# An encoder step in float32: right sides of three norms built between the sums of the next pair, a phase's first factors applied at the end of its first unit

## The chip, the cores and the metric

One core of a Trainium2 chip runs the whole program. The metric is the device time of one execution in microseconds, the median over several. Lower is better. The engines are TensorE (PE), VectorE (DVE), ScalarE (ACT), GpSimd (POOL), and SyncE (SP), whose queue issues all transfers between DRAM and the on-chip memory, in order.

## The reference

One inference step of a four-layer trunk for 1024 prompt tokens and 8 × 16 sample tokens, 1152 columns together, D = 1024 rows, all in float32. After the attention layer (its output projection is `w_ao`) the same residual `x` goes through a feed-forward layer, a gated short convolution and another feed-forward layer:

```python
def swiglu(h, wg, wu, wd):
    return (jax.nn.silu(h @ wg) * (h @ wu)) @ wd

def conv_mixer(h, w_in, conv_w, w_out, conv_state):
    gate_b, gate_c, u = jnp.split(h @ w_in, 3, axis=-1)
    xin = gate_c * u
    ...
    y = (gate_b * conv) @ w_out

xp = xp + mp                                          # attention or conv
xp = xp + swiglu(rms_norm(xp, norm_ffn[i]), w_ffn_gate[i], w_ffn_up[i], w_ffn_down[i])
```

`rms_norm` multiplies each column by the root of its mean square's inverse, and each row by a gain.

## The kernel before

**Products.** Every float32 factor is split into a high and a low half (`part`, `halve`: ScalarE casts the high half, VectorE subtracts it to get the low one), and a product is three matmuls: high by high, high by low, low by high. `x` lies as eight tiles of 128 x 1152 (rows by columns), `x[0]` to `x[7]`. A matmul has 384 columns (a third of a tile) or 288 (a quarter).

**Phases.** After attention come, in this order: the last chunk of the output projection (`pairs` with `w_aol`, two of the heads), `gates` of layer 0 (22 units), `down` of layer 0, `conv` (12 units), `w_cout` (`down` again), `gates` of layer 1, `down_last`. `gates` and `conv` write their results `y` to DRAM (`yd`), and the `down` phases load them back in chunks: DOWN = (2, 8, 8, 4) and COUT = (2, 2, 4) blocks of 128 rows of `y` per chunk. In a chunk `pairs` goes through four pairs of `x` tiles, (0, 4), (1, 5), (2, 6), (3, 7); for each of six groups (two tiles, three thirds) TensorE sums nk products, three matmuls each, and VectorE adds the group to `x` (L1130).

**Units.** A unit (`unit`) is a 2 x 2 block product done with seven products instead of eight. Each has a left side from the weights (`a11`, `s1` to `s4` and so on) and a right side from `x` (`t1` to `t4`, `b11`, `b21`, `b22`; a trace calls them tt1, tb11 and so on with h or l for the half), in the order t2, t1, b11, b21, t3, t4, b22. Each is 24 matmuls of 288 columns, 12 for each half `s`, 168 in a unit. Right sides are built once per phase, and all units use them. There are 28 slots for halves (NT = 20 of their own and NY = 8 shared with `y`).

**A norm.** In the last chunk before `gates` or `conv`, `sides(st, x, j)` is called after each pair: it builds that pair's share of the right sides from `x` (ScalarE `v`, VectorE L899 and L869), and squares both tiles in halves of 576 columns (ScalarE L932), which GpSimd adds to `ssq` (L933). Sides without a free slot go to `late` and are built in `end_sides`. The norm's factor is not in the right sides; it is a row `rb`, multiplied into the products (`first`, `second` and `end` in the callback `sink`). `rb` comes from `sums` (18 small matmuls over `ssq`), `rstd` (a chain of some 15 short VectorE instructions) and `spread`: high diagonals from ScalarE (L276), low ones from GpSimd (L278), 18 matmuls of 384 columns, three copies.

**What sets the order.** The program is recorded through a scheduling layer, which may exchange neighbours on an engine; then each engine runs its own list in order. `tick` is called after each half of a product and runs what `late` holds when its count of ticks is over: `sums` two ticks into the first unit, `spread` three later, so ahead of the unit's first use of `rb`:

```python
        self.late.append([2, sums])
        ...
            self.late.append([3, lambda: spread(r)])
```

**The names around it.** `g` and `u` of a unit come from rings of three buffers (`wide`, ZBUFS = 3). `row` gives full-width rows from a ring of three. `xd` is `x` in DRAM: `x` is spilled there before `conv`, since `conv` uses the `x` buffers for `xi`, and loaded back for `w_cout` (L1206). A `conv` unit's channel ends with three taps and `cv` times `rb` (L1094, GpSimd, 128 x 1152).

## Time and profile before

| what | value |
|---|---|
| time, median of 3 runs | 2751.44 us (2749.30 to 2755.26) |
| profiled execution, its own time | 2751.61 us |
| its span | 2749.5 us |
| TensorE busy | 2623.1 us, 95% |
| VectorE busy | 1736.9 us, 63% |
| ScalarE busy | 929.4 us, 34% |
| GpSimd busy | 660.4 us, 24% |
| mean granted TensorE clock | 0.975 |
| DMA | 276.28 MB, mean 100 GB/s |

The profiled execution's time is 2.1 us more than the span from its first to its last instruction. Busy shares are means over phases of different kinds; the granted clock is a share of the full 2.4 GHz, so 0.5 is the lower level of 1.2 GHz. Matmuls overlap in the records, so a pace is read from start to start or from counts in a stretch.

### The profile page before, as it was taken

The page shows a single profiled execution, that of the slowest core. Times are in us where ns is not written, and L with a number is a line of the kernel's source. Part 1 is how long each engine was busy: PE and PEld are TensorE (multiplying, and loading weights), DVE is VectorE, ACT ScalarE, POOL GpSimd, SP SyncE. Part 2 cuts the span into 40 slices and gives each one's busy share as a digit, 9 for nine tenths or more (in the row PEclk, how much of TensorE's full clock was granted, in tenths as well). Part 3 has the DMA queues.
Part 4 walks back from the last instruction along what each step waited for, and adds up shares of the span by engine and source line. Part 5 has one row for each costly group of instructions (what it writes and reads, how often), then busy time and mean ns, then how long its engine had stood idle before and what let it go on. Part 6 is the DMA issues. An engine that isn't in the chain of part 4 may idle for free. (4 is left out here: it accounts for less than half of the span.)

```text
span 2749.5 us, 45135 instructions
## 1 busy us (share of the span) xinstructions
PE 2623.1 (95%) x17440; PEld 2575.7 (94%) x17440; DVE 1736.9 (63%) x3535; ACT 929.4 (34%) x1765; POOL 660.4 (24%) x699
## 2 busy tenths in 40 slices
PE   7999999999599999999999799989899999999998
PEld 6899999989599999999999799989799999999997
DVE  7667766687866666665327776677766666673325
ACT  5555444453422222232104321223422222241114
POOL 6334233320322222220002333321322222220002
PEclk9999999999799999999999899999899999999999
DMA  6655555561022222244212122261122222253211
GB/s 195 181 170 167 165 179 172 162 215 42 20 93 73 76 73 79 76 134 138 72 39 90 37 78 61 65 186 30 41 88 75 74 73 73 76 174 95 72 39 69
DMA packets 176952, 276.28 MB, mean 100 GB/s; under 512 B 38241, under 2 KB 107745, under 8 KB 176737
## 3 DMA queue, kind: packets, MB, share of 16 engines
q1 hardware_dynamic: 176736, 273.40, 32.0%
q8 instruction: 137, 2.24, 0.3%
q14 instruction: 79, 0.64, 0.1%
HBM read 201.95 MB, written 71.38 MB: 99 GB/s over the span
## 5 line engine op out<-in xcount | busy, mean ns | idle before, releaser
L868 ACT CAST h<-r 128x512 fp32r<-128x512 f32 x492 | 302.9, 617 | 999.8 <-PE ps_g L996 457.3
L869 DVE TENSOR_TENSOR l<-r,h 128x512 fp32r<-128x512 f32 x492 | 348.5, 709 | 119.5 <-ACT h L868 104.6
L163 PE MATMUL ps_g<-yh,h 128*128 128x384 f32 x1152 | 387.2, 336 | 3.8 <-DVE g L1015 3.8
L164 PE MATMUL ps_g<-yl,h 128*128 128x384 f32 x1152 | 387.9, 337 | 0.0
L165 PE MATMUL ps_g<-yh,l 128*128 128x384 f32 x1152 | 386.0, 335 | 0.0
L1041 POOL TENSOR_TENSOR u<-u,rb 128x576 f32<-128x576 f32 x88 | 146.9, 1670 | 665.7 <-DVE u L999 658.4
L1130 DVE TENSOR_TENSOR x<-ps_g,x 128x384 f32<-128x384 f32 x264 | 141.6, 553 | 237.0 <-PE ps_g L165 236.8
L163 PEld LDWEIGHTS ps_g<-yh,h 128*128 128x128 f32 x1152 | 216.7, 188 | 5.0 <-DVE g L1015 4.7
L165 PEld LDWEIGHTS ps_g<-yh,l 128*128 128x128 f32 x1152 | 216.6, 188 | 0.0
L164 PEld LDWEIGHTS ps_g<-yl,h 128*128 128x128 f32 x1152 | 216.4, 188 | 0.0
L163 PE MATMUL ps_g<-hh,wh 128*128 128x384 f32 x544 | 193.8, 357 | 10.1 <-ACT hh L197 6.7
L967 DVE TENSOR_TENSOR r<-r,r 128x512 f32<-128x512 f32 x224 | 174.8, 780 | 40.6 <-DMA r<-in_w_gu 19.2
L164 PE MATMUL ps_g<-hl,wh 128*128 128x384 f32 x544 | 185.7, 341 | 1.5 <-DVE hl L198 1.4
L165 PE MATMUL ps_g<-hh,wl 128*128 128x384 f32 x544 | 185.1, 340 | 0.8 <-DVE wl L155 0.8
L933 POOL TENSOR_TENSOR ssq<-ssq,sq 128x576 f32<-128x576 f32 x42 | 75.6, 1821 | 409.4 <-ACT sq L932 409.3
L1045 DVE TENSOR_TENSOR g<-g,u 128x576 f32<-128x576 f32 x88 | 67.1, 762 | 143.1 <-ACT g L1044 143.0
L995 PE MATMUL ps_g<-tb21h,h 128*128 128x288 f32 x448 | 137.0, 306 | 18.7 <-ACT u L1002 18.7
L995 PE MATMUL ps_g<-tt2h,h 128*128 128x288 f32 x448 | 133.1, 298 | 9.9 <-ACT tt2h L868 9.9
L997 PE MATMUL ps_g<-tb21h,l 128*128 128x288 f32 x448 | 137.1, 306 | 0.0
L996 PE MATMUL ps_g<-tb21l,h 128*128 128x288 f32 x448 | 136.6, 305 | 0.0
L995 PE MATMUL ps_g<-tt3h,h 128*128 128x288 f32 x448 | 135.2, 302 | 1.2 <-DVE g L1003 1.2
L995 PE MATMUL ps_g<-tt1h,h 128*128 128x288 f32 x448 | 133.6, 298 | 1.5 <-ACT tt1h L868 1.5
(277 smaller groups left out, 7555.7 us busy)
## 6 DMA issues: line engine op xcount, KB each, us to landing
r<-in_w_gu SPq DMA_DIRECT2D x176, 256.0 KB, 2.7
y<-yd SPq DMA_DIRECT2D x52, 576.0 KB, 4.6
yd<-g SPq DMA_DIRECT2D x96, 288.0 KB, 2.6
r<-in_w_down SPq DMA_DIRECT2D x88, 256.0 KB, 2.6
wr<-in_w_in SPq DMA_DIRECT2D x24, 512.0 KB, 4.2
r<-in_w_cin SPq DMA_DIRECT2D x48, 256.0 KB, 2.7
kc<-in_ck SPq DMA_DIRECT2D x16, 512.0 KB, 4.3
vc<-in_cv SPq DMA_DIRECT2D x16, 512.0 KB, 4.0
```

Source lines behind the costliest of these rows:

```text
L163: nc.tensor.matmul(ps, wh, xh, start=(j == 0), stop=False)
L164: nc.tensor.matmul(ps, wh, xl, start=False, stop=False)
L165: nc.tensor.matmul(ps, wl, xh, start=False, stop=(j == n - 1))
L868: self.nc.scalar.copy(hi, raw)
L869: self.nc.vector.tensor_tensor(lo, raw, hi.bitcast(F32), ALU.subtract)
L933: nc.gpsimd.tensor_tensor(st["ssq"][:, cs], st["ssq"][:, cs], sq, ALU.add)
L967: nc.vector.tensor_tensor(t, x_, y, ALU.add)
L995: nc.tensor.matmul(ps, w[0][:, k, :], hi, start=(new and k == 0), stop=False, skip_group_check=True)
L996: nc.tensor.matmul(ps, w[0][:, k, :], lo, start=False, stop=False, skip_group_check=True)
L997: nc.tensor.matmul(ps, w[1][:, k, :], hi, start=False, stop=(k == 3), skip_group_check=True)
L1041: nc.gpsimd.tensor_tensor(u, u, self.cols(rb, s), ALU.mult)
L1130: nc.vector.tensor_tensor(x[m][:, c], ps, x[m][:, c], ALU.add)
```

## The change

Six edits; names and lines are those of the changed kernel where it is spoken of alone.

1. `sides` builds nothing at once. It returns three lists: `now` (sides that have slots), `then` (sides without) and squares. `pairs` runs `now`, and the squares of the pair before, in portions after each of the next pair's six adds. What is left is run after the last pair, sides first, squares last.
2. `square` squares a whole tile (128 x 1152) on ScalarE, and VectorE adds it to `ssq`; GpSimd's 14 half adds of each norm are gone.
3. `sums` comes six ticks into the phase; then 18 diagonals are made in one go into two rows, and `spread` comes at tick 15, which is in the second unit. The first unit (`first`) therefore doesn't use `rb`: ScalarE copies its product instead, and `rest` multiplies `g` (VectorE) and `u` (GpSimd) by `rb` after the spread and then runs the unit's `end`.
4. The first unit begins with those products that don't need the last pair's sides (three of four k blocks of t2 and t1, two of four of b11: 48 matmuls). Its left sides are built before the last pair's right sides. The first pair of a norm's chunk runs all its `y` but the last first, for its six groups.
5. The chunks: `w_ao[0]` (heads 0 and 1 of the second map) is no longer a separate accumulation but part of `w_aol`, which now has four blocks; layer 0's `down` has (2, 6, 8, 6), layer 1's stays; `w_cout` has (2, 6). NY is 11 and NT 17, the same 28 slots.
6. `x` is spilled to `xd` in the chunk before `gates` of layer 1, too. Where `x` is spilled, its tiles 0, 4, 1 and 5 become slots for right sides as soon as their own sides are built; `fetch_x` loads `x` back before `w_cout` and before `down_last`, in the order 0, 4, 1, 5, 2, 6, 3, 7.

The conv unit's and the gate's callbacks (`sink`) become functions `end` that run after both halves are multiplied; both of the gate's writes to `yd` now stand there. In the diff a line that is only "..." marks what is left out.

```diff
-NY = 8
+NY = 11
-DOWN = (2, 8, 8, 4)
-COUT = (2, 2, 4)
+DOWN = ((2, 6, 8, 6), (2, 8, 8, 4))
+COUT = (2, 6)
-NT = 20
+NT = 17
-SUMS = 5
+SUMS = 6
+SPREAD = 15
...
-        y0 = heads(self.od[0], (0, 1))
+        y = heads(self.od[0], (0, 1))
         self.accumulate(pp, x, y1, i["w_ao"][3], step=loom.step)
         loom.drain()
-        y1 = heads(self.od[0], (2, 3))
-        self.accumulate(pp, x, y0, i["w_ao"][0], banks="gs")
+        y += heads(self.od[0], (2, 3))
...
+        now = [lambda: vee("v"), one, two, lambda: halve("t2", "r2"), lambda: halve("t1", "r1"), four, lambda: halve("t4", "r4")]
...
             if self.side(st, p, z) is not None:
-                do()
+                now.append(do)
             else:
-                st["late"].append(do)
...
-                    sq = flat("zu", "sq")
-                    nc.scalar.activation(sq, xm[:, cs], AF.Square)
-                    nc.gpsimd.tensor_tensor(st["ssq"][:, cs], st["ssq"][:, cs], sq, ALU.add)
...
+            sq = self.row("sq")
+            nc.scalar.activation(sq, xm, AF.Square)
+            nc.vector.tensor_tensor(st["ssq"], st["ssq"], sq, ALU.add)
+
+    def roots(self, st):
...
+            dg = [self.row("diag", F32R) for _ in range(2)]
+            for j in range(9):
+                c = slice(j * P, (j + 1) * P)
+                nc.scalar.activation(dg[0][:, c], self.ident, AF.Copy, scale=parts[:, 0, j:j + 1].bitcast(F32))
+                nc.gpsimd.tensor_scalar(dg[1][:, c], self.ident, parts[:, 1, j:j + 1].bitcast(F32), 1.0, ALU.mult, ALU.mult)
+            self.late.append([SPREAD - SUMS, lambda: spread(dg)])
...
+            for do in st["rest"]:
+                do(rb)
+        self.late.append([SUMS, sums])
...
+        if first:
+            for n in range(3):
+                for s in range(2):
+                    products(n, s, range(2 if n == 2 else 3))
...
+                    if first:
+                        nc.scalar.copy(zg[s][:, 0], ps)
+                    else:
+                        vt.tensor_tensor(zg[s][:, 0], ps, by()[0][:, self.head(s)], ALU.mult)
...
+        if first:
+            def rest(s, rb):
+                nc.vector.tensor_tensor(zg[s], zg[s], self.cols(rb, s), ALU.mult)
+                nc.gpsimd.tensor_tensor(zu[s], zu[s], self.cols(rb, s), ALU.mult)
+                end(s, zg[s], zu[s])
...
+            early = nk - 1 if st is not None and j == 0 else 0
+            if early:
+                for g in groups:
+                    products(*g, range(early))
+            for n, (z, b, ps) in enumerate(groups):
+                products(z, b, ps, range(early, nk))
+                self.tick()
+                c = slice(b * BLK, (b + 1) * BLK)
+                xm = x[j + 4 * z][:, c]
+                nc.vector.tensor_tensor(xm, ps, xm, ALU.add)
+                for _ in range(-(-len(todo) // (6 - n))):
+                    todo.pop(0)()
             if st is not None:
-                self.sides(st, x, j)
+                if j == KT // 2 - 1:
+                    st["split"] = self.left_sides(*st["first"])
+                now, late, square = self.sides(st, x, j)
+                if st["spill"] and j < 2:
+                    self.free += ["x", "x"]
+                squares.append(square)
+                todo = now + (squares.pop(0) if j or st["spill"] else [])
+                then.append(late)
...
+    def fetch_x(self):
+        self.free = [t for t in self.free if t != "x"]
+        x = [self.xtile("x") for m in range(KT)]
+        for j in range(KT // 2):
+            for m in (j, j + 4):
+                self.nc.sync.dma_start(x[m], self.xd[m])
+        return x
...
-            st = self.begin_sides(3, pp, False)
+            st = self.begin_sides(3, pp, gu(1)(0), True)
             self.down(pp, x, i["w_cout"], COUT, st)
-            self.gates(pp, 1, st)
-            self.down_last(pp, x, i["w_down"][1], DOWN)
+            self.gates(pp, gu(1), st)
+            x = self.fetch_x()
+            self.down_last(pp, x, i["w_down"][1], DOWN[1])
```

What the scheduling layer makes of it is seen in the lists of the engines. First VectorE, norm 1, at the last pair of the last chunk, before the change (`x_1701` and `x_1705` are the tiles 3 and 7, `ps_g` a group's sum, `r` an intermediate, `tt` and `tb` right sides):

```order
L1130 TENSOR_TENSOR x_1701_7325<-ps_g_9028,x_1701_7325 128x384
L869 TENSOR_TENSOR tt1l_8985<-r_2081_8990,tt1h_8984 128x576
L1130 TENSOR_TENSOR x_1701_7325<-ps_g_9036,x_1701_7325 128x384
L869 TENSOR_TENSOR tt4l_8987<-r_2083_8994,tt4h_8986 128x576
L1130 TENSOR_TENSOR x_1701_7325<-ps_g_9044,x_1701_7325 128x384
L1130 TENSOR_TENSOR x_1705_7329<-ps_g_9052,x_1705_7329 128x384
L1130 TENSOR_TENSOR x_1705_7329<-ps_g_9060,x_1705_7329 128x384
L1130 TENSOR_TENSOR x_1705_7329<-ps_g_9068,x_1705_7329 128x384
L899 SCALAR_TENSOR_TENSOR r_2102_9078<-x_1701_7325,gains,v_9076 128x576
L899 SCALAR_TENSOR_TENSOR tb11l_9003<-x_1701_7325,gains,tb11h_9002 128x576
L899 SCALAR_TENSOR_TENSOR r_2103_9080<-x_1705_7329,gainsn,r_2102_9078 128x576
```

The same place after the change (`r_9020` and the like are left sides of the first unit, `l_9025` a low half of one):

```order
L1183 TENSOR_TENSOR x_1701_7325<-ps_g_8912,x_1701_7325 128x384
L869 TENSOR_TENSOR tt1l_8895<-r_2073_8931,tt1h_8894 128x576
L990 TENSOR_TENSOR r_9020<-r_9016,r_9018 128x512
L1183 TENSOR_TENSOR x_1705_7329<-ps_g_8913,x_1705_7329 128x384
L869 TENSOR_TENSOR tt4l_8897<-r_2075_8965,tt4h_8896 128x576
L990 TENSOR_TENSOR r_9022<-r_9014,r_9016 128x512
L1183 TENSOR_TENSOR x_1705_7329<-ps_g_8914,x_1705_7329 128x384
L869 TENSOR_TENSOR l_9025<-r_9020,h_9024 128x512
L990 TENSOR_TENSOR r_9028<-r_9022,r_9018 128x512
L898 SCALAR_TENSOR_TENSOR r_2097_9052<-x_1701_7325,gains,v_9050 128x576
L1183 TENSOR_TENSOR x_1705_7329<-ps_g_8915,x_1705_7329 128x384
```

Right sides of the pair before and left sides of the unit now stand between the adds of the last pair.

GpSimd from the last `ssq` adds of norm 1 to the second half of the first unit, before:

```order
L933 TENSOR_TENSOR ssq_8829<-ssq_8829,sq_9100 128x576
L933 TENSOR_TENSOR ssq_8829<-ssq_8829,sq_9103 128x576
L278 TENSOR_SCALAR diag_9264<-ident,rp_9257 128x128 x3
L278 TENSOR_SCALAR diag_9279<-ident,rp_9272 128x128 x3
L278 TENSOR_SCALAR diag_9294<-ident,rp_9287 128x128 x3
L1041 TENSOR_TENSOR u_9303<-u_9303,rb_9122 128x576
L1041 TENSOR_TENSOR u_9320<-u_9320,rb_9122 128x576
```

And after the change, in the first and second unit (`u_9189`, `u_9247` are the first unit's, `u_9489` the second's):

```order
L967 TENSOR_SCALAR diag_9227<-ident,rp_2132_9223 128x128 x9
L1078 TENSOR_TENSOR u_9189<-u_9189,rb_9405 128x576
L1078 TENSOR_TENSOR u_9247<-u_9247,rb_9405 128x576
L1062 TENSOR_TENSOR u_9489<-u_9489,rb_9405 128x576
L1062 TENSOR_TENSOR u_9506<-u_9506,rb_9405 128x576
```

The adds are gone, the nine low diagonals stand together, and the first unit's products follow them instead of standing in its middle.

SP's queue where `conv` ends and `w_cout` begins, before (`y` loads from `yd`, `x` from `xd`):

```order
L1206 DMA x_20069<-xd 128x1152
L1206 DMA x_20070<-xd 128x1152
L858 DMA r_20255<-in_w_cout 128x512
L1114 DMA y_20311<-yd 128x1152
L1114 DMA y_20317<-yd 128x1152
L858 DMA r_20321<-in_w_cout 128x512
L1103 DMA yd<-u_19931 256x1x288
L858 DMA r_20375<-in_w_cout 128x512
L1103 DMA yd<-u_19948 256x1x288
L1206 DMA x_20071<-xd 128x1152
L1106 DMA yd<-g_19930 256x1x288
```

And after the change:

```order
L1217 DMA x_19982<-xd 128x1152
L1217 DMA x_19986<-xd 128x1152
L858 DMA r_20171<-in_w_cout 128x512
L1153 DMA y_20239<-yd 128x1152
L1153 DMA y_20245<-yd 128x1152
L858 DMA r_20261<-in_w_cout 128x512
L858 DMA r_20267<-in_w_cout 128x512
L858 DMA r_20273<-in_w_cout 128x512
L1217 DMA x_19983<-xd 128x1152
L1145 DMA yd<-u_19847 256x1x288
L1145 DMA yd<-u_19864 256x1x288
```

Four `x` loads instead of six stand ahead of the first two `y`, and the last `y` writes stand together.

## Rows read from the trace of the kernel before

**Rows 1.** The page: busy time, share of the span and instructions by engine.

```profile
PE 2623.1 (95%) x17440; PEld 2575.7 (94%) x17440; DVE 1736.9 (63%) x3535; ACT 929.4 (34%) x1765; POOL 660.4 (24%) x699
```

**Rows 2.** Stretches: length, busy time of each engine (instructions), TensorE clock, DMA share, GB/s.

```profile
645.30:669.30 24.00, 24.00 (x141) 24.00 (x140) 15.67 (x29) 2.53 (x4) 0.00 (x0) 1.00 0.23 77
669.30:727.00 57.70, 31.81 (x163) 30.36 (x161) 56.67 (x74) 33.59 (x53) 24.76 (x14) 0.76 0.03 10
...
761.00:783.20 22.20, 22.20 (x170) 22.20 (x169) 14.31 (x25) 6.30 (x11) 4.82 (x5) 1.00 0.32 101
1507.60:1556.60 49.00, 35.32 (x193) 33.11 (x192) 34.57 (x62) 20.91 (x40) 17.14 (x17) 0.76 0.14 50
...
1936.70:1984.60 47.90, 34.78 (x195) 32.29 (x194) 35.37 (x63) 20.02 (x39) 17.87 (x18) 0.79 0.11 33
```

**Rows 3.** Timeline, TensorE, norm 1: start, length, instruction, idle before and releaser.

```profile
699.02 0.66 PE L163 MATMUL ps_g<-oh,h 128*128 128x384 f32 x1 [9.39 <-DVE x L1130]
...
723.15 1.01 PE L948 MATMUL ps_n<-ones,ssq 128*128 128x1 f32 x4 [15.66 <-POOL ssq L933]
```

**Rows 4.** Timeline, TensorE, norm 2 (the first three) and norm 3.

```profile
1518.20 0.85 PE L995 MATMUL ps_g<-tt2h,h 128*128 128x288 f32 x2 [4.95 <-ACT tt2h L868]
...
1524.67 0.49 PE L948 MATMUL ps_n<-ones,ssq 128*128 128x1 f32 x3 [1.54 <-POOL ssq L933]
...
1537.60 0.69 PE L286 MATMUL ps_n<-diag,onesr 128*128 128x384 f32 x1 [4.37 <-ACT diag L276]
...
1966.57 0.69 PE L286 MATMUL ps_n<-diag,onesr 128*128 128x384 f32 x1 [4.27 <-ACT diag L276]
```

**Rows 5.** Timeline, GpSimd, the last sums of squares of norm 1.

```profile
717.40 7.51 POOL L933 TENSOR_TENSOR ssq<-ssq,sq 128x576 f32<-128x576 f32 x4 [3.44 <-ACT sq L932]
```

**Rows 6.** Groups of VectorE by shape: count, busy us, mean ns, idle before.

```profile
L869 DVE TENSOR_TENSOR l<-r,h 128x512 fp32r<-128x512 f32 x492 | 348.5, 709 | 119.5 <-ACT h L868 104.6
...
L1130 DVE TENSOR_TENSOR x<-ps_g,x 128x384 f32<-128x384 f32 x264 | 141.6, 553 | 237.0 <-PE ps_g L165 236.8
...
L869 DVE TENSOR_TENSOR yl<-y,yh 128x1152 fp32r<-128x1152 f32 x52 | 72.7, 1403 | 27.4 <-ACT yh L868 27.4
...
L899 DVE SCALAR_TENSOR_TENSOR r<-x,gainsn,r 128x576 f32<-128x576 f32 x24 | 19.4, 809 | 0.0
...
L869 DVE TENSOR_TENSOR tt2l<-r,tt2h 128x576 fp32r<-128x576 f32 x12 | 9.0, 749 | 0.0
```

**Rows 7.** Timeline, VectorE, sides of norm 1.

```profile
694.58 1.95 DVE L899 SCALAR_TENSOR_TENSOR r<-x,gains,v 128x576 f32<-128x576 f32 x1
...
728.12 1.53 DVE L899 SCALAR_TENSOR_TENSOR tb22l<-x,gains,tb22h 128x576 fp32r<-128x576 f32 x2
```

**Rows 8.** Timeline, GpSimd, low diagonals of norm 1.

```profile
739.82 2.99 POOL L278 TENSOR_SCALAR diag<-ident,rp 128x128 fp32r<-128x128 f32 x6 [14.91 <-DVE rp L269]
744.17 1.06 POOL L278 TENSOR_SCALAR diag<-ident,rp 128x128 fp32r<-128x128 f32 x3 [1.35 <-PE ps_n L286]
```

**Rows 9.** Timeline, VectorE, GpSimd and TensorE, the second chain of conv.

```profile
1592.29 3.03 DVE L967 TENSOR_TENSOR r<-r,r 128x512 f32<-128x512 f32 x1
...
1591.73 3.04 POOL L1094 TENSOR_TENSOR cv<-cv,rb 128x1152 f32<-128x1152 f32 x1 [2.84 <-DVE cv L1093]
...
1596.38 0.40 PE L995 MATMUL ps_g<-tb21h,h 128*128 128x288 f32 x1 [2.15 <-ACT u L1002]
...
1598.05 0.44 PE L996 MATMUL ps_g<-tb21l,h 128*128 128x288 f32 x1
1598.29 0.44 PE L997 MATMUL ps_g<-tb21h,l 128*128 128x288 f32 x1
```

**Rows 10.** Waits of TensorE, 1580 to 1870 us: in total, times, longest us.

```profile
PE ps_g L995 <- ACT u L1002: 12.8, 6, 2.2
```

**Rows 11.** Timeline, TensorE, beginning of `w_cout`.

```profile
1837.47 0.44 PE L163 MATMUL ps_g<-yh,h 128*128 128x384 f32 x1 [2.22 <-DVE g L1015]
```

**Rows 12.** DMA issues, 1810 to 1840 us: count, KB each, median us to landing.

```profile
x<-xd SPq DMA_DIRECT2D x7, 576.0 KB, 12.7
```

More of the change, by code (lines that the diff above doesn't have):

```diff
@@ L218, in norm_sum @@
                 self.norm_end(st, b)()
-            elif st["new"] is not None:
-                self.late.append([SUMS, lambda: self.late.append([1, self.norm_end(st, b)])])
             elif b < NB - 1:
@@ L869, in halve, with begin_sides @@
         self.nc.vector.tensor_tensor(lo, raw, hi.bitcast(F32), ALU.subtract)
-    def begin_sides(self, gi, pp, spill):
-        return {"gi": gi, "pp": pp, "t": {}, "late": [], "ssq": None, "spill": spill, "v": {}}
+    def begin_sides(self, gi, pp, first, spill=False):
+        return {"gi": gi, "pp": pp, "t": {}, "ssq": None, "first": first, "spill": spill, "split": None, "rest": None}
     def side(self, st, p, z, need=False):
@@ L981, in unit, with products @@
         for n in range(PARTS):
-            if order[n][0] in raws:
-                split[order[n][0]] = self.part(raws[order[n][0]])
-        zone = {}
-        zg, zu = [None, None], [None, None]
+            wn = self.ORDER[n][0]
+            if wn in raws:
+                split[wn] = self.part(raws[wn])
+        return split, raws
+    def unit(self, pp, st, weights, by, end, last=False):
+        nc = self.nc
+        first = "rb" not in st
+        if st["split"] is not None:
+            split, raws = st["split"]
+            st["split"] = None
+        else:
+            split, raws = self.left_sides(*weights)
+        order = self.ORDER
+        zone, zg, zu = {}, [None, None], [None, None]
+        tail = lambda s: slice(HALF + s * SUB, HALF + (s + 1) * SUB)
+        vt = nc.vector
+        neg = lambda t, z: vt.scalar_tensor_tensor(t, z, -1.0, t, ALU.mult, ALU.subtract)
+        def products(n, s, ks):
+            wn, p, zn = order[n]
+            w = split[wn]
+            new = (zn, s) not in zone
+            if new:
+                zone[zn, s] = self.psum(pp, "g", (P, 512))[:, :SUB]
+            ps = zone[zn, s]
+            for k in ks:
+                hi, lo = (t[:, k % 2, s * SUB:(s + 1) * SUB] for t in self.side(st, p, k // 2))
+                nc.tensor.matmul(ps, w[0][:, k, :], hi, start=(new and k == 0), stop=False, skip_group_check=True)
+                nc.tensor.matmul(ps, w[0][:, k, :], lo, start=False, stop=False, skip_group_check=True)
+                nc.tensor.matmul(ps, w[1][:, k, :], hi, start=False, stop=(k == 3), skip_group_check=True)
+        if first:
+            for n in range(3):
+                for s in range(2):
+                    products(n, s, range(2 if n == 2 else 3))
@@ L986, in unit @@
         for n, (wn, p, zn) in enumerate(order):
-            w = split[wn]
             for s in range(2):
-                new = (zn, s) not in zone
-                if new:
-                    zone[zn, s] = self.psum(pp, "g", (P, 512))[:, :SUB]
+                products(n, s, range(4) if not first or n > 2 else range(2 if n == 2 else 3, 4))
                 ps = zone[zn, s]
-                for k in range(4):
-                    hi, lo = (t[:, k % 2, s * SUB:(s + 1) * SUB] for t in self.side(st, p, k // 2))
-                    nc.tensor.matmul(ps, w[0][:, k, :], hi, start=(new and k == 0), stop=False, skip_group_check=True)
-                    nc.tensor.matmul(ps, w[0][:, k, :], lo, start=False, stop=False, skip_group_check=True)
-                    nc.tensor.matmul(ps, w[1][:, k, :], hi, start=False, stop=(k == 3), skip_group_check=True)
@@ L1022, in unit @@
                 split[ahead] = self.part(raws[ahead])
+        if first:
[3 more added lines that the diff above has]
+                end(s, zg[s], zu[s])
+            st["rest"] = [lambda rb, s=s: rest(s, rb) for s in range(2)]
+            st["rb"] = None
     def cols(self, t, s):
@@ L1135, in pairs @@
         if st is not None:
-            self.end_sides(st)
+            names = [p for p, _ in then[-1]]
+            for p in names:
+                for late in then:
+                    for q, do in late:
+                        if q == p:
+                            do()
+            for square in squares:
+                for do in square:
+                    do()
+            self.roots(st)
+    def fetch_x(self):
[5 more added lines that the diff above has]
+        return x
     def down(self, pp, x, wsrc, chunks, st):
@@ L1317 @@
         o[name] = nc.dram_tensor(f"out_{name}", shape, F32, kind="ExternalOutput").ap()
-    i["w_down"] = [[i[f"w_down{l}{n}"] for n in range(len(DOWN))] for l in range(2)]
+    i["w_down"] = [[i[f"w_down{l}{n}"] for n in range(len(DOWN[l]))] for l in range(2)]
     i["w_cout"] = [i[f"w_cout{n}"] for n in range(len(COUT))]
```

222 lines of the change are left out of this document (106 added, 116 removed).

## The prediction

> **What bounds the kernel now.** I read the page's busy times first: TensorE is busy 95% of the span [rows 1], so time can only be won where it stands or runs at half clock. The table of stretches shows where [rows 2]. The stretch from 645.3 is a steady one: 139 matmuls of 384 columns (two of the 141 counted began earlier) in 24.0 us, 0.174 us each; a whole unit of gates (168 matmuls of 288 columns) takes the 22.2 us from 761.0, 0.132 us each, both at clock 1.00. At this pace a phase's first unit needs 22.2 us, 3.1 us for the 18 matmuls of `spread` and about 2 us for the sums, 27.3 in all. The three changes of phase need far more:
> - Norm 1 (the chunk `w_aol` from 669.3 to the end of the first unit at 761.0): 91.7 us for 144 × 0.174 + 27.3 = 52.4, an excess of 39.3.
> - Norm 2 (1507.6 to 1556.6): 49.0 for 27.3, excess 21.7.
> - Norm 3 (1936.7 to 1984.6): 47.9 for 27.3, excess 20.6.
>
> Together 81.6 us; half clock (0.76 to 0.79 mean in these rows) is part of it. The waits say what is late. In norm 1 TensorE stands 9.39 us for the add of `x`, which VectorE has queued behind right sides, and 15.66 us for the last GpSimd add of `ssq` [rows 3]. In norm 2 it stands 4.95 us for `tt2h` of the last pair and 4.37 for the diagonals, in norm 3 4.27 for the diagonals [rows 4]. GpSimd's adds follow one another, four in 7.51 us [rows 5], and beside them a VectorE side takes 1.95 us [rows 7] where its group's mean is 0.81 [rows 6].
>
> **The change, part by part.** The profiled run took 2751.61 us, 2.1 above its span and 0.2 above the median of 2751.44, so the sum is made from 2751.6.
>
> *Norm 1.* The two heads of `w_ao[0]` join the last chunk: 144 matmuls move from ahead of it into it, so it begins at 645.3 and has 288 matmuls, 50.1 us. Three of four heads run first for pair 0, so the first `x` add comes after 57 matmuls, at 655.2; from then on VectorE is the one to count. Between its first add and the last `ssq` add the new order has 24 adds of 0.553 us, 28 sides of 0.809, 16 halves of 0.749, 8 of 0.709, 4 left-side adds near 0.709 and 7 `ssq` adds of 128x1152, for which I take the 1.403 of the equally wide `yl` [rows 6]: 13.3 + 22.7 + 12.0 + 5.7 + 2.8 + 9.8 = 66.3 us. These are durations of single instructions; back to back they start closer (two sides in 1.53 us [rows 7]), which makes it about 60. So `ssq` is done at 715 to 721. TensorE could be there at 645.3 + 50.1 + 96 × 0.132 = 708.1. It will stand 7 to 13 us before or at the sums, and behind them in its order stands the rest of the unit. I take 8, near the lower end: the means of [rows 6] hold cases that a GpSimd add slowed, and no such add is left. The diagonals come next: from the sums VectorE's root chain, with what is interleaved, is some 10 us by the same prices, then nine high diagonals on ScalarE and, beside them and longer, nine low ones on GpSimd (six in 2.99 us [rows 8]): 4.5 us more. Their `spread` now stands 85 matmuls (11.2 us) later, against the 11.9 us that sums to spread took in norm 2 [rows 4]. So about 2.5 us of wait is left, and I add 2.5 us of half clock for both (1.5 follow a wait of 2.15 us in the conv phase, below). Excess 13 instead of 39.3: a gain of 26.3. Bounds: excess 6 (all at the lower prices, no half clock) to 25.
>
> *Norms 2 and 3.* The last chunk has six `y` (before: four), 108 matmuls or 18.8 us per pair. VectorE's same 66 us now lie beside 75 us of pairs and the 12.7 us up to the sums, no longer behind them. Of the last pair only `tt2`, `tt1` and `b11` are on the path: from its last add some six instructions, 5.3 us, against 48 matmuls of cover (6.3 us). If that cover is gone, each us late is a us lost. Left are about 2.5 us at the spread and 1.5 of half clock, excess 4 each (1 to 12): gains 17.7 and 16.6.
>
> *First unit's factors at its end.* `g` times `rb` (two of 576 on VectorE), `u` times `rb` (two on GpSimd): they stand beside second-unit work on engines that are idle a third of a unit (VectorE 14.3 busy of 22.2 us [rows 2]). They cost nothing unless the three buffers of `g` and `u` run out: the fourth is wanted after six groups of the second unit, and the first is freed earlier by two or three us, by my count. Cost 0, bound 3 us a phase.
>
> *Conv.* The chains `cv` times `rb` stay on GpSimd: 3.04 us there, 3.03 for the left-side add on VectorE beside it, ScalarE's `u` stands behind that add's half, and TensorE waits 2.15 us and then runs at half clock for some 3 us (0.24 us from start to start in place of 0.13) [rows 9], about 1.5 us lost; 12.8 us of wait in six such places [rows 10]. A seventh, the first, lies at 1566. The diff leaves the order of the six; the first chain now follows the second unit's spread and may lie elsewhere: gain 0 to 3.7, I take 2.
>
> *x through DRAM.* Eight loads before `w_cout` as before, now four of them behind the first `y` pair; so the 2.22 us that TensorE stands there [rows 11] stay, within ±6; price 0. For `w_down` 1 eight more loads and for norm 3 eight writes: four loads stand early in the gates, four among the `y` loads at the end. In a crowd a load lands after 12.7 us [rows 12], and what is behind it in SP's queue is late by its start; I take 2 us of loss (0 to 6).
>
> *One fewer chunk in `w_cout`, 24 fewer adds in each of two places*: VectorE work beside a busy TensorE; nothing.
>
> Sum: −26.3 − 17.7 − 16.6 − 2 + 0 + 2 = −60.6, so 2751.6 − 60.6 = **2691 us**. Norm 1's 8 us is the softest term.
>
> **A rule weighed.** The rows: six low diagonals on GpSimd took 2.99 us beside VectorE's adds, 0.50 us each; three in 1.06 us are 0.35 each [rows 8]; and a two-input add beside a GpSimd product took 3.03 [rows 9]. The Trainium skill (SBUF — State Buffer, "Who interferes with whom") says that a VectorE instruction with two SBUF inputs and a GpSimd instruction that reads SBUF exclude each other for the whole instruction. The product's row agrees; the diagonals' row does not show a whole wait for each. By that row the sum stays 2691; whole waits are the second rival.
>
> **Rivals.**
> - *VectorE becomes the bound inside the pairs.* Sides now stand between the adds that free TensorE's banks; before, such a queue cost 9.39 us once [rows 3]. For it: in norm 1 60 to 66 us of VectorE work meet 53 us of TensorE. Against: norms 2 and 3 have 88 us. If every pair is late, excesses of 25, 12 and 12: gain 14.3 + 9.7 + 8.6 = 32.6, about 2719.
> - *Low diagonals late.* If each of the nine waits for one VectorE instruction of 0.749 [rows 6], they take 9 × (0.35 + 0.75) = 9.9 instead of 4.5 us: 5.4 us more at each spread, 16 in all, 2707. For it rows 9, against it rows 8. This is what the rule named above would do.
> - *More is won.* Excesses of 6, 1, 1 and the first conv chain gone: gain 33.3 + 20.7 + 19.6 + 3.7 − 2 = 75, 2676.
> - *Slower.* A load of `x` waits in SP's queue until a side slot is free, and weights and `y` stand behind it in order. Side slots in `x` buffers come free only in a phase's last unit. If the queue stands so before `w_cout` and `w_down`, TensorE waits for `y`. The price is up to a unit (22.2 us) for each of the two; to outweigh 60 us of gain it must be three units or more. Against it: the loads that stand early need other buffers.
>
> **How the numbers follow.** Forecast 0.60, VectorE the bound 0.19, low diagonals 0.09, more won 0.06, slower 0.04, a gain lost to several of these so that it lies within 0.2% (5.5 us, about what a measurement of this kernel can tell) 0.02. The likeliest, with norm 1 between its bounds and the others in the middle, lies between 2684 and 2703; the range of 2668 to 2720 takes in the first three rivals, and below them the 6 us of `w_cout`. Faster 0.94, same 0.02, slower 0.04.
>
> **What would show it.** Right: no GpSimd add of `ssq`, sides at 0.7 to 0.8 us throughout, one wait of 7 to 13 us near the sums of norm 1, in norms 2 and 3 no wait for `tt2h` and a few us at the diagonals, six conv waits of 2 us left. Wrong: waits for `x` adds inside the pairs, for `u` or `g` buffers in second units, or for `y` behind `x` loads.

## The result

The changed kernel takes 2702.37 us, the kernel before 2751.96 us beside it; 49.6 us less by the medians; the ratio, taken over all runs, is 0.9815 with a 95% interval of 0.9802 to 0.9828. The forecast was 2691. A second timing of the same kernel on another chip (the run "again" below) gave 0.9785 (0.9764 to 0.9805), so a kernel's ratio is known to about 0.3% only, and small edits are read from stretches of the profile rather than from the total.

The page's busy line of the changed kernel:

```profile
PE 2609.2 (97%) x17440; PEld 2568.3 (95%) x17440; DVE 1715.0 (64%) x3498; ACT 935.1 (35%) x1761; POOL 581.2 (22%) x651
```

TensorE is busy for 14 us less than in [rows 1] in a span that is 50.3 us shorter. The stretches that answer to [rows 2]: from attention's last matmul to the third unit of norm 1, the first two units of norm 2, the other nine of `conv` up to the last, the last `conv` unit with `w_cout`, and the first three units of norm 3:

```profile
645.00:761.70 116.70, 102.55 (x651) 100.83 (x650) 92.92 (x156) 58.30 (x94) 11.77 (x14) 0.94 0.20 63
1486.30:1540.30 54.00, 49.96 (x361) 49.16 (x360) 46.03 (x84) 21.01 (x43) 16.99 (x18) 0.97 0.18 52
1540.30:1766.20 225.90, 211.38 (x1515) 209.75 (x1514) 164.16 (x263) 47.48 (x83) 70.42 (x60) 0.95 0.24 69
1766.20:1897.70 131.50, 125.80 (x747) 125.05 (x746) 92.97 (x141) 46.60 (x66) 15.16 (x9) 0.97 0.42 135
1897.70:1978.00 80.30, 74.59 (x530) 73.93 (x530) 55.73 (x103) 30.84 (x58) 16.36 (x18) 0.94 0.33 108
```

The same stretches of the kernel before took 139.1, 75.3, 223.9, 129.9 and 92.4 us. So norm 1 gave 22.4 us, norm 2 21.3 and norm 3 12.1; `conv` and `w_cout` took 2.0 and 1.6 back, the end 0.8, and the parts ahead of norm 1 and between norms 1 and 2 together 1.1. In norms 2 and 3 the first units alone take 24.3 us each, where [rows 2] has 49.0 and 47.9; the units behind them take 3.5 us (norm 2) and 11.4 us (norm 3) longer than before, of which 1.1 each is the `spread` that moved there. The waits of TensorE in the span (in total, times, longest us) show what is left:

```profile
PE ps_g L1033 <- ACT u L1048: 22.2, 12, 2.2
PE ps_g L1170 <- ACT h L868: 9.3, 1, 9.3
PE ps_g L1033 <- DVE u L1057: 7.6, 4, 3.9
...
PE ps_g L1033 <- DVE u L1022: 4.5, 1, 4.5
...
PE ps_g L1034 <- DVE tb11l L898: 1.8, 1, 1.8
```

No wait for `ssq`, for a diagonal of these norms or for `tt2h` is left; those for 9.39 and 15.66 us of [rows 3] and for 4.95, 4.37 and 4.27 of [rows 4] are gone. In their place stand 9.3 us at the beginning of norm 1, 3.9 and 2.9 us in second units, and 4.5 us at the end of `conv`.

**The new wait of norm 1.** SP's queue in the timeline, then TensorE's first matmul of the merged chunk:

```profile
646.64 0.45 SPq L570 DMA_DIRECT2D o<-olo  x1
648.91 0.80 SPq L790 DMA_DIRECT2D o<-o  x2
649.82 7.13 SPq L858 DMA_DIRECT2D r<-in_w_aol  x8
```

```profile
654.60 0.69 PE L1170 MATMUL ps_g<-oh,h 128*128 128x384 f32 x1 [9.32 <-ACT h L868]
```

The chunk's weights (`in_w_aol`) are issued behind the transfers of the last heads, which wait for attention's end. Before, 24 us of matmuls of `w_ao[0]` stood between; now nothing does, and TensorE waits for the high halves of the weights.

**VectorE in norm 1.** Its first add and its last `ssq` add:

```profile
666.61 3.16 DVE L1183 TENSOR_TENSOR x<-ps_g,x 128x384 f32<-128x384 f32 x6 [8.70 <-PE ps_g L1172]
...
724.89 1.34 DVE L949 TENSOR_TENSOR ssq<-ssq,sq 128x1152 f32<-128x1152 f32 x1
```

From 666.6 to 726.2 are 59.6 us, where the prediction had 60 to 66. No side is slowed beside them now: two take 1.53 us throughout.

**The new wait of norm 3.** ScalarE, then VectorE, then TensorE in the second unit of layer 1's gates (its third begins at 1952.1):

```profile
1940.26 1.15 ACT L868 CAST yh<-y 128x1152 fp32r<-128x1152 f32 x1 [6.45 <-DMA y<-yd]
```

```profile
1941.44 1.36 DVE L869 TENSOR_TENSOR yl<-y,yh 128x1152 fp32r<-128x1152 f32 x1 [4.83 <-ACT yh L868]
1942.72 0.45 DVE L1057 TENSOR_TENSOR u<-ps_g,u 128x288 f32<-128x288 f32 x1
```

```profile
1943.22 0.61 PE L1033 MATMUL ps_g<-tt4h,h 128*128 128x288 f32 x1 [3.92 <-DVE u L1057]
```

ScalarE stands 6.45 us at the cast of a `y` that is still on its way from DRAM, VectorE behind it at that cast's low half, and the `u` that frees TensorE's bank stands behind both. The `y` is that of the phase's first unit, which is written only after the second unit's `spread`.

**The wait ahead of `w_cout`.** SP's queue, ScalarE and TensorE in the last `conv` unit:

```profile
1771.63 8.51 SPq L1217 DMA_DIRECT2D x<-xd  x4
1781.18 1.07 SPq L1153 DMA_DIRECT2D y<-yd  x2
```

```profile
1790.36 1.15 ACT L868 CAST yh<-y 128x1152 fp32r<-128x1152 f32 x1 [10.73 <-DMA y<-yd]
```

```profile
1793.33 0.61 PE L1033 MATMUL ps_g<-tb22h,h 128*128 128x288 f32 x1 [4.48 <-DVE u L1022]
```

The `y` is issued behind four loads of `x` and is at hand 9.2 us after its issue; ScalarE stands 10.73 us at its cast, and TensorE behind VectorE behind that. The kernel before stood 2.22 and 1.53 us at the beginning of `w_cout` itself.

### The profile page after: what moved, and what is told of

Same layout as the page of the kernel before. It is cut to its first block, busy times and chain, and to the rows that moved or that the text cites. A ratio compares the mean times of both kernels' runs of the same rounds, so it can differ in the third digit from the quotient of the medians.

```text
span 2699.2 us, 45160 instructions
## 1 busy us (share of the span) xinstructions
PE 2609.2 (97%) x17440; PEld 2568.3 (95%) x17440; DVE 1715.0 (64%) x3498; ACT 935.1 (35%) x1761; POOL 581.2 (22%) x651
## 5 line engine op out<-in xcount | busy, mean ns | idle before, releaser
L869 DVE TENSOR_TENSOR l<-r,h 128x512 fp32r<-128x512 f32 x496 | 359.2, 726 | 127.0 <-ACT h L868 111.8
L1171 PE MATMUL ps_g<-yl,h 128*128 128x384 f32 x1152 | 386.7, 336 | 0.0
L1062 POOL TENSOR_TENSOR u<-u,rb 128x576 f32<-128x576 f32 x98 | 158.2, 1634 | 743.2 <-DVE u L1022 725.9
L1183 DVE TENSOR_TENSOR x<-ps_g,x 128x384 f32<-128x384 f32 x240 | 129.4, 552 | 235.3 <-PE ps_g L1172 234.8
L1171 PEld LDWEIGHTS ps_g<-yl,h 128*128 128x128 f32 x1152 | 216.5, 188 | 0.0
L1172 PEld LDWEIGHTS ps_g<-yh,l 128*128 128x128 f32 x1152 | 216.4, 188 | 0.0
L1033 PE MATMUL ps_g<-tt4h,h 128*128 128x288 f32 x448 | 134.5, 300 | 7.6 <-DVE u L1057 7.6
L1033 PE MATMUL ps_g<-tb22h,h 128*128 128x288 f32 x448 | 132.9, 297 | 4.5 <-DVE u L1022 4.5
L1034 PE MATMUL ps_g<-tb21l,h 128*128 128x288 f32 x448 | 136.1, 304 | 0.0
L1034 PE MATMUL ps_g<-tt3l,h 128*128 128x288 f32 x448 | 134.2, 300 | 0.0
```

Of the source, the lines that this page charges most:

```text
L869: self.nc.vector.tensor_tensor(lo, raw, hi.bitcast(F32), ALU.subtract)
L1033: nc.tensor.matmul(ps, w[0][:, k, :], hi, start=(new and k == 0), stop=False, skip_group_check=True)
L1034: nc.tensor.matmul(ps, w[0][:, k, :], lo, start=False, stop=False, skip_group_check=True)
L1062: nc.gpsimd.tensor_tensor(zu[s], zu[s], self.cols(by()[1], s), ALU.mult)
L1171: nc.tensor.matmul(ps, w[q][0][:, e, :], ys[k][1][0][:, c], start=False, stop=False, skip_group_check=True)
L1172: nc.tensor.matmul(ps, w[q][1][:, e, :], ys[k][0][0][:, c], start=False, stop=(k == nk - 1), skip_group_check=True)
```

## The experiments

All are the changed kernel with the edit shown. The table gives the lengths of the five stretches named above, in us, from the profile of each, and the ratio to the kernel before with its interval; the changed kernel and the same kernel again stand first behind the kernel before.

| kernel | norm 1 | norm 2 | conv | w_cout | norm 3 | ratio |
|---|---|---|---|---|---|---|
| before | 139.1 | 75.3 | 223.9 | 129.9 | 92.4 | 1 |
| changed | 116.7 | 54.0 | 225.9 | 131.5 | 80.3 | 0.9815 (0.9802 to 0.9828) |
| again | 120.9 | 54.1 | 223.0 | 131.8 | 80.3 | 0.9785 (0.9764 to 0.9805) |
| bridge | 117.7 | 53.8 | 227.2 | 132.3 | 79.4 | 0.9791 (0.9775 to 0.9808) |
| own_ao | 126.2 | 53.8 | 217.1 | 132.1 | 79.7 | 0.9811 (0.9790 to 0.9831) |
| no_early | 128.9 | 54.3 | 217.0 | 131.8 | 76.4 | 0.9829 (0.9807 to 0.9851) |
| ssq_pool | 126.5 | 54.9 | 226.5 | 132.1 | 79.0 | 0.9843 (0.9830 to 0.9857) |
| no_defer | 124.5 | 58.1 | 222.1 | 132.4 | 82.8 | 0.9843 (0.9823 to 0.9862) |
| no_portions | 116.1 | 53.8 | 220.0 | 132.7 | 77.6 | 0.9785 (0.9771 to 0.9799) |
| old_cout | 120.5 | 54.1 | 220.2 | 132.9 | 78.3 | 0.9796 (0.9781 to 0.9812) |
| unit_order | 121.9 | 54.1 | 226.5 | 132.6 | 72.3 | 0.9774 (0.9750 to 0.9798) |
| taps_dve | 117.2 | 50.8 | 215.1 | 131.9 | 80.3 | 0.9761 (0.9747 to 0.9776) |
| two_mends | 120.6 | 52.2 | 216.4 | 132.0 | 72.6 | 0.9753 (0.9734 to 0.9772) |
| three_mends | 120.3 | 52.2 | 215.7 | 132.0 | 74.1 | 0.9753 (0.9740 to 0.9767) |

### The same kernel again

> The changed kernel itself, beside the three that follow and on the same chip: 0.981 to 0.983 of the kernel before by both theories; it shows how far one profile's stretches differ from another's (norm 1 within 4 us, the others within 2).

Norm 1 differs by 4.2 us and `conv` by 2.9 between two profiles of one kernel, norms 2 and 3 by 0.1 at most. In norm 1 the difference lies behind the sums: up to them the two take 81.4 and 82.0 us, behind them 35.3 and 38.9, without a wait in either, at clock 0.98 and 0.60 in the first 10 us. So the whole of norm 1 is to be read with 4 us of doubt, the part up to the sums (81.0 to 83.0 us in the eight kernels that change nothing there or only the portions) with 2, and `conv`, where kernels without an edit in it lie between 217.0 and 227.2, with 10.

### bridge

```diff
+        self.accumulate(pp, x, y[:2], i["w_ao"][0], banks="gs", ms=(0, 1, 4, 5))
...
+            k0 = 2 if st is not None and st["gi"] == 1 and j in (0, 1) else 0
```

> Two of the four blocks of the attention chunk go back into a separate accumulation for the tiles 0, 1, 4 and 5 only (72 matmuls, 12.5 us, twelve more VectorE adds); all else as changed. Theory one, the chunk's first weights stand behind the last heads' transfers in SP's queue and nothing covers them now: the wait of 9.3 us at 645 falls under 1 us, the second unit starts 6 us earlier (3 to 9), and the time falls as much, to about 2696. Rival, VectorE is the bound of norm 1 and has 6.6 us more to do: the wait moves to the first unit, time as changed within 2 us.

The wait at the beginning is gone, and norm 1 is as long as before the edit, 117.7 us. The waits of TensorE in it now (L1171 and L1173 are the pairs, L1034 the units; the wait for `h` stands at the first unit's beginning):

```profile
PE ps_g L1034 <- ACT h L869: 2.6, 1, 2.6
PE ps_g L1173 <- DVE l L870: 2.3, 2, 1.9
PE ps_g L1171 <- DVE x L1185: 1.3, 1, 1.3
PE ps_n L959 <- DVE ssq L950: 1.2, 1, 1.2
```

From the stretch's beginning, the adds of the last chunk begin 4.4 us earlier than in the changed kernel's profile, VectorE ends its `ssq` 2.0 us earlier, and the sums come 2.0 us earlier (79.4 us; 2.6 against the second profile). That gain is lost again behind the sums, in the part that is 3.6 us apart in two profiles of one kernel. So most of the filled wait comes back as others, for VectorE and for halves of weights: nearer to the rival's mechanism, with 2 to 3 us left of the 6 of theory one. The ratio doesn't tell this kernel from the changed one.

### own_ao

```diff
-        y += heads(self.od[0], (2, 3))
+        y = heads(self.od[0], (2, 3))
+        self.accumulate(pp, x, y0, i["w_ao"][0], banks="gs")
...
-    d["w_aol"] = paired(a["w_attn_out"][0], 0, 4)
+    d["w_aol"] = paired(a["w_attn_out"][0], 2, 2)
```

> Heads 0 and 1 of the second map accumulate by themselves ahead of the last chunk again (144 matmuls, 24 more VectorE adds); all else as changed. Theory one, VectorE sets the end of norm 1: its 55 us of sides and adds then lie beside 25 us of pairs and 12.7 of the first unit instead of 50 and 12.7, so although the wait of 9.3 us for the weights goes, norm 1 is 8 to 15 us longer. Rival, the merged chunk only traded one wait for another: norm 1 within 3 us.

Norm 1 is 9.5 us longer than in the profile of the changed kernel and 5.3 longer than in its second one; the wait of 9.3 us is gone and one of 15.4 has come, for a high half of a left side at the first unit's beginning:

```profile
PE ps_g L1034 <- ACT h L869: 15.4, 1, 15.4
```

That is within theory one's 8 to 15 us against one profile and short of it against the other; the rival's 3 us doesn't hold in either, and up to the sums norm 1 takes 89.1 us instead of 81.4 and 82.0. The profiled execution's total (2702.15 us, the changed kernel's 2701.08) doesn't show it, since its `conv` was the shortest but one of the ten kernels without an edit there.

### no_early

```diff
-        if first:
-            for n in range(3):
-                for s in range(2):
-                    products(n, s, range(2 if n == 2 else 3))
...
-                    st["split"] = self.left_sides(*st["first"])
...
-            early = nk - 1 if st is not None and j == 0 else 0
+            early = 0
```

> Without the early products of the first unit and of the first pair, and with the first unit's left sides built after the right sides, as before; deferral, portions, chunks and adds as changed. Theory one, the last pair's first sides are ready some 6 us after its last add and nothing covers that: TensorE waits 4 to 6 us for tt2 or a left side and runs at half clock after it, each norm 5 to 8 us longer, 20 in all, about 2720. Rival, the sides recorded during the pairs leave so little behind that the waits are under 2 us a norm.

Norm 1 is 8 to 12 us longer, but by another wait than expected, that for `ssq`:

```profile
722.42 2.90 PE L958 MATMUL ps_n<-ones,ssq 128*128 128x1 f32 x13 [13.19 <-DVE ssq L949]
```

In TensorE's list the sums of norm 1 stand 96 matmuls earlier here, right behind the last matmul of the chunk, and `ssq` isn't done until 13.2 us later; the first unit's products, which the changed kernel takes in that time, come behind. In norms 2 and 3 nothing is lost (54.3 and 76.4 us; the first units take 24.5 and 24.4): the rival holds there. The list shows why: their sums stand at the same place in both kernels, with 72 of the first unit's matmuls between the chunk's last and them, only in another order. So this edit takes the early products back in norm 1 and hardly in the other two.

### ssq_pool

```diff
-            nc.vector.tensor_tensor(st["ssq"], st["ssq"], sq, ALU.add)
+            nc.gpsimd.tensor_tensor(st["ssq"], st["ssq"], sq, ALU.add)
```

> Only the adds of squares (1152 wide, seven per norm) go back from VectorE to GpSimd. Theory one, the gain came from the order (sides, early products, the sums later), so the adds matter only where VectorE is short: norm 1 slower by 3 to 9 us (each GpSimd add holds a VectorE side for up to 3 us, VectorE saves 1.4 each), norms 2 and 3 within 2 us. Rival, GpSimd's adds beside the sides were the main cause of the time before: each norm 7 us or more slower, over 20 in all.

Norm 1 is 5.6 to 9.8 us longer, norm 2 0.9, norm 3 1.3 shorter. Theory one holds in norms 2 and 3 and against the second profile in norm 1 (9.8 is above its 9): GpSimd's adds matter where VectorE is short. Each of the seven adds of norm 1 has a VectorE instruction beside it that takes 2.76 to 3.21 us instead of 0.7 to 0.8, as here:

```profile
716.58 2.84 POOL L949 TENSOR_TENSOR ssq<-ssq,sq 128x1152 f32<-128x1152 f32 x1 [6.75 <-ACT sq L948]
716.84 3.19 DVE L898 SCALAR_TENSOR_TENSOR r<-x,gains,v 128x576 f32<-128x576 f32 x1
```

### no_defer

```diff
-SUMS = 6
-SPREAD = 15
+SUMS = 1
+SPREAD = 7
...
-        if first:
-            def rest(s, rb):
...
-                    if not first:
+                    if True:
```

> The first unit is multiplied by rb in itself again (sums one tick and spread seven ticks into it, 33 matmuls apart), the 48 early products and all else as changed. Theory one, the chain from sums to diagonals takes 12 us and only 4.4 us of matmuls cover it: TensorE waits 7 us or more for the diagonals in each norm, with half clock after it; against that the late first y of norm 3 (waits of 3.9 and 1.8 us in the third and fourth unit) and the crowded second unit of norm 2 go. Norm 1 slower by 9, norm 2 by 4, norm 3 by 2 us, about 2717 in all. Rival, deferring gives back all it wins: within 3 us of the changed kernel.

Norm 1 is 3.6 to 7.8 us longer, norm 2 4.1, norm 3 2.5: the sum (10 to 14) is near the 15 expected, the waits are others. Diagonals cost about 1 us each, and TensorE stands for `u`, whose copy on ScalarE comes behind a half that waits 8.03 us for VectorE. The waits of TensorE in norm 2, in total, times, longest:

```profile
PE ps_g L1032 <- ACT u L1047: 6.4, 2, 6.3
PE ps_n L285 <- POOL diag L968: 0.9, 1, 0.9
```

### no_portions

```diff
+                while todo:
+                    todo.pop(0)()
```

> Right sides are recorded at once after their pair, as in the kernel before, all other edits kept. Theory one, norms 2 and 3 have 18.8 us of TensorE per pair and don't need the portions, norm 1 has 12.5 and does: norms 2 and 3 within 1.5 us each, norm 1 slower by 4 to 12 us, for adds that stand behind sides. Rival, the portions are the core of the gain: every norm 8 us or more slower, 25 in all.

No norm is longer, norm 3 is 2.7 us shorter. Both theories are wrong for norm 1: even there, where an add was expected to stand behind sides, the portions aren't needed. The adds of a pair stand behind the sides in VectorE's list here too, but TensorE has six banks to fill meanwhile; that this is the reason is read from the code and was not tried.

### old_cout

```diff
-COUT = (2, 6)
+COUT = (2, 2, 4)
...
-            st = self.begin_sides(3, pp, gu(1)(0), True)
+            st = self.begin_sides(3, pp, gu(1)(0), False)
...
-            x = self.fetch_x()
             self.down_last(pp, x, i["w_down"][1], DOWN[1])
```

> w_cout in chunks of 2, 2, 4, and x neither spilled nor its buffers lent in norm 3; norms 1 and 2 as changed. Theory one, 12.5 us of TensorE per pair in place of 18.8 don't cover VectorE in norm 3: the stretch from its first to its fourth unit is 6 to 10 us longer, w_cout's own begin within 2 us. Rival, the early products and late sums are enough by themselves: the stretch as changed within 2 us, and the tail 1 us shorter without the loads of x.

Norm 3 is 2.0 us shorter, not longer, `w_cout` 1.4 longer, the end behind norm 3 0.2 shorter. By these sums the rival would hold. But the stretch has two parts that went opposite ways, its first unit and the two behind it; the changed kernel first, then old_cout:

```profile
1897.70:1922.00 24.30, 24.30 (x188) 24.30 (x188) 22.06 (x49) 14.99 (x31) 3.11 (x8) 1.00 0.52 166
1922.00:1978.00 56.00, 50.30 (x344) 49.63 (x344) 33.67 (x54) 15.85 (x27) 13.24 (x11) 0.91 0.25 83
```

```profile
1901.00:1933.40 32.40, 28.32 (x186) 27.28 (x187) 29.94 (x58) 18.24 (x35) 1.97 (x4) 0.89 0.15 43
1933.40:1979.30 45.90, 45.90 (x344) 45.71 (x343) 31.94 (x52) 13.95 (x26) 14.90 (x15) 1.00 0.33 103
```

The first unit is 8.1 us longer, as theory one has it, and TensorE stands in it again, for VectorE and for ScalarE's copies:

```profile
PE ps_g L1034 <- DVE tb11l L898: 1.8, 1, 1.8
PE ps_g L1033 <- ACT u L1048: 1.2, 2, 0.8
PE ps_n L958 <- DVE ssq L949: 1.1, 1, 1.1
```

The second and third are 10.1 us shorter, because the wait for the late `y` isn't there: ScalarE casts it 484 us after the norm's beginning, at the end of the gates, instead of 43. So the bigger last chunk with the lent `x` buffers wins 8 us in norm 3's first unit, and in this order of units its early cast of the late `y` loses 10; unit_order keeps the first and mends the second. Which of the two, chunk or buffers, does what isn't told apart.

### unit_order

```diff
-        for f in range(FT):
+        for f in order:
...
+            order = (2, 0, 1) + tuple(range(3, FT))
+            st = self.begin_sides(3, pp, gu(1)(2), True)
```

> The gates of layer 1 begin with unit 2, then 0, 1, 3 and on; all else as changed. Theory one, in norm 3 the deferred first unit writes its y late, ScalarE's cast of it is queued ahead of halves that TensorE needs: with another unit first, the waits of 3.9 and 1.8 us and their half clock go, the stretch from the first to the fourth unit falls from 80.3 to about 74 us. Rival, the order on ScalarE follows the same estimate for whichever unit is loaded first: the wait moves by a unit, 80 us as before.

Norm 3 takes 72.3 us, 8.0 less, at clock 1.00:

```profile
1905.60:1977.90 72.30, 70.39 (x530) 69.95 (x530) 54.85 (x102) 29.89 (x57) 16.27 (x18) 1.00 0.35 111
```

Theory one. One wait for `u` of 1.9 us is left in this stretch; in the later gates there are two, 4.3 us in all, where the changed kernel has one of 1.8.

### taps_dve

```diff
-                    nc.gpsimd.tensor_tensor(v, v, st["rb"], ALU.mult)
+                    nc.vector.tensor_tensor(v, v, st["rb"], ALU.mult)
```

> Only cv times rb (1152 wide, eight times) goes from GpSimd to VectorE. Theory one, in conv the GpSimd product holds a two-input VectorE add for 3 us and ScalarE's copy of u waits behind it: the add takes 0.7 us again, the product 1.4 us, the six waits of 2.1 us for u and the half clock after them (3.9 us each) go, time falls by 18 to 24 us, to about 2681. Rival, VectorE's queue is what is late, whoever holds it: 1.4 + 0.7 us instead of 3.0 leaves waits of about 1 us with their half clock, time falls by 6 to 10.

The product takes 1.35 us on VectorE, and the left-side adds behind it 1.28 for two, where [rows 9] had 3.03 for one:

```profile
1598.16 1.35 DVE L1138 TENSOR_TENSOR cv<-cv,rb 128x1152 f32<-128x1152 f32 x1
...
1600.04 1.28 DVE L990 TENSOR_TENSOR r<-r,r 128x512 f32<-128x512 f32 x2
```

The stretch runs at full clock, and the waits for `u` stay, five of them 1.6 us instead of 2.2 (the second line counts from 1500 to 1770, where the changed kernel has 14.5 us in seven):

```profile
1539.00:1754.10 215.10, 202.52 (x1515) 200.65 (x1514) 154.72 (x269) 47.50 (x83) 54.91 (x55) 1.00 0.26 73
```

```profile
PE ps_g L1033 <- ACT u L1048: 12.6, 8, 2.5
```

`conv` takes 215.1, 216.4 and 215.7 us in the three kernels that have this edit, and between 217.0 and 227.2 (mean 222.6) in the ten changed ones without it: 7 us on the mean, and norm 2 is 2 to 3 us shorter. The medians of bridge and no_portions, timed beside it, are 6.6 us higher. That lies at the rival's numbers. GpSimd's hold was a part of the wait; the rest stayed with the product on VectorE. Most of the 7 us is clock, though: own_ao and no_early, with the old product but also at 1.00 in this stretch, took 217.1 and 217.0, 2 us more than here. That the shorter waits keep the clock up is not shown by three kernels.

### two_mends and three_mends

Both take the diffs of unit_order and taps_dve, three_mends also that of no_portions.

> The changed kernel with unit 2 first in layer 1's gates and with cv times rb on VectorE. Theory one, the two sit in different stretches (norm 3, conv) and add up: 8 us and 13 us less, 0.974 to 0.975 of the kernel before, about 2681. Rival, one frees time that the other's waits take back: no better than 0.976.

> As the last one, and the sides recorded at once after their pair, without portions. Theory one, portions gain nothing in any norm: within 3 us of the last one. Rival, the 6 us by which the kernel without portions was faster are theirs: 0.972 of the kernel before.

Norm 3 keeps most of its gain, `conv` too. Both ratios are 0.9753, just short of theory one's 0.974 to 0.975 and better than its rival's 0.976, which lies within both intervals; so the two are not told apart. The intervals end at 0.9772 and 0.9767: clear of the changed kernel's first timing (from 0.9802), not quite of its second (from 0.9764), which ran beside them. The third edit adds nothing that the ratio shows.

## Why the prediction was right, and where it was not

The time lay 11 us above the forecast and inside the range. By its steps:

- *The bound.* "Time can only be won where TensorE stands or runs at half clock": right: the three norms gave 55.8 us, and everything else took 5.5 back. One number in it was wrong, as it is in the part on the kernel before: `spread` has six matmuls (two halves, three thirds), 1.1 us and not 18 with 3.1. The excesses were therefore 2 us larger than stated.
- *Norm 1, forecast 26.3, measured 22.4 (18.2 in the second profile).* The mechanism was right: VectorE sets the end, and its 59.6 us agree with the lower of the two sums. The step that failed is "the first `x` add comes after 57 matmuls, at 655.2": it came at 666.6, because the chunk's weights are late. The prediction counted the matmuls that moved and not the transfer that they had covered. What it expected as a wait of 8 us at the sums came as a wait of 9.3 us for weights: VectorE began that much later, and TensorE lost the time ahead of it instead of behind it, so that the size came out near by some luck. own_ao, no_early and ssq_pool show that each of merged chunk, early products (with the early left sides) and `ssq` on VectorE is worth 5 to 12 us here. bridge shows that filling the weights' wait alone gives 2 to 3 us up to the sums: VectorE's end moves by about half of what its first add does.
- *Norm 2, forecast 17.7 and 2 for the first chain, measured 21.3.* Right in size, by two errors against each other: the first unit has none of the 4 us of excess left, and its successor loses 3.5. The wait at the diagonals (2.5 us) did not come; 2.9 and 1.1 us in the second unit came instead, where the first unit's `end` and its conv chain crowd VectorE.
- *Norm 3, forecast 16.6, measured 12.1.* Here the step on the first unit's factors failed: "cost nothing unless the three buffers run out". The buffers never ran out, but the first unit's `y` is late, and ScalarE's queue holds its cast ahead of what TensorE needs. The price, set at 0 with a bound of 3, was 11.4 us in the second and third units, the moved spread's 1.1 among them; unit_order, which gives 8.0 us back, shows it. That the sum was off by only 4.5 is luck: the first unit won 23.6, with none of its 4 us of excess left.
- *Why the old waits of norms 2 and 3 went.* The prediction put it to the six blocks of the last chunk and the 48 early products. For norm 3 old_cout shows the first: with the smaller chunk, and without the lent buffers, TensorE stands in the first unit again, and it is 8.1 us longer. The early products were hardly taken back in norms 2 and 3, as the list of no_early shows. ssq_pool costs their first units 1.1 us each, no_portions nothing, no_defer 2.8 and 4.3. The bigger chunk of norm 2 was not taken back by any run. In the trace before, VectorE was 8 us behind at the first unit's beginning of norm 2 (its last add came at 1515.4, the unit began at 1507.6), now it is level with it; that the chunk did this there too is likely from norm 3 and stays open.
- *Conv, `w_cout`, the loads of `x`* came within 2 us each of the zero, zero and 2 that were set. The six waits of 2 us stayed. But one of the prediction's signs of being wrong was there, a `y` behind loads of `x`: the 4.5 us ahead of `w_cout`, in place of 2.22 and 1.53.
- *The rivals.* VectorE did not bind inside the pairs (no wait for an `x` add is in the list of waits, and no_portions shows that the portions aren't the reason). The low diagonals did not hold TensorE up, but not for the reason given: [rows 8] was read as a mean, and the trace takes it apart. Before, in norm 1, the first of the six took 1.26 us beside two VectorE instructions with two SBUF inputs, the other five 1.75 us together:

```profile
739.82 1.26 POOL L278 TENSOR_SCALAR diag<-ident,rp 128x128 fp32r<-128x128 f32 x1 [14.91 <-DVE rp L269]
739.63 0.69 DVE L967 TENSOR_TENSOR r<-r,r 128x512 f32<-128x512 f32 x1
740.24 0.69 DVE L869 TENSOR_TENSOR l<-r,h 128x512 fp32r<-128x512 f32 x1
```

And after the change, in norm 2, the first, the second to seventh and the eighth of nine, with VectorE's instructions beside them:

```profile
1508.26 1.20 POOL L967 TENSOR_SCALAR diag<-ident,rp 128x128 fp32r<-128x128 f32 x1 [18.21 <-DVE rp L962]
1509.43 2.10 POOL L967 TENSOR_SCALAR diag<-ident,rp 128x128 fp32r<-128x128 f32 x6
1511.51 0.80 POOL L967 TENSOR_SCALAR diag<-ident,rp 128x128 fp32r<-128x128 f32 x1
```

```profile
1508.01 0.69 DVE L990 TENSOR_TENSOR r<-r,r 128x512 f32<-128x512 f32 x1
1508.61 0.68 DVE L869 TENSOR_TENSOR l<-r,h 128x512 fp32r<-128x512 f32 x1
1509.21 0.45 DVE L1065 TENSOR_TENSOR g<-ps_g,g 128x288 f32<-128x288 f32 x1
1511.31 0.77 DVE L869 TENSOR_TENSOR l<-r,h 128x512 fp32r<-128x512 f32 x1
```

A diagonal takes 0.37 us alone or beside an instruction that reads a PSUM bank, and one that begins while an instruction with two SBUF inputs runs ends some 0.2 us after that. The Trainium skill (SBUF — State Buffer, "Who interferes with whom") has such a pair contend for an exclusive lock, and the trace agrees. The rival's condition therefore held, and its count failed: two of the nine met such an instruction (three in norm 1, one in norm 3), and the nine took 4.40 us instead of 9.9.

## What to carry to other kernels

When matmuls are moved away from a place, look for what they covered: the next phase's weights, in the queue that issues them, behind transfers that wait. Work that is put off makes its product late too; whatever loads that product has to be moved behind the new time, or the in-order engine that casts it stops for it. And where several edits aim at one wait, take each back by itself, and read its worth in the smallest stretch that holds it, when the totals of two timings differ by more than the edit: here the portions could go without a loss, and another edit looked worthless over three units because it won 8 us in the first and lost 10 in the next two. A mean over a few instructions hides a wait that only some of them meet.

## What the runs showed of the hardware

A wait of the same length is followed by half clock in one place and not in another. In no_portions TensorE stood 2.22 us before 1603.05 and 2.19 us before 1629.28, in the same place of two units; the clock (the number just ahead of the DMA share) in the 3 us after each:

```profile
1603.20:1606.20 3.00, 3.00 (x16) 3.00 (x17) 2.97 (x8) 0.62 (x1) 0.00 (x0) 0.63 0.06 11
1629.40:1632.40 3.00, 3.00 (x23) 3.00 (x24) 2.97 (x8) 0.62 (x1) 0.00 (x0) 1.00 0.04 8
```

Such waits make `conv` some 9 us longer or shorter between kernels that are equal there: with six of them (2.0 to 2.2 us) each, own_ao ran the stretch at 1.00 in 217.1 us and the changed kernel at 0.95 in 225.9. GpSimd and a VectorE instruction with two SBUF inputs wait for each other, whichever began first holding the other up: VectorE's took 3.03 us behind a product in [rows 9] and 3.06 in the changed kernel's `conv` (at 1549.12), and a short diagonal 0.80 to 1.20 us instead of 0.37 behind VectorE's.
